# A feed-forward block's weight sums and gated differences change places between PSUM and SBUF, and their low halves change engines

## The chip, the cores and the metric

The kernel runs on one core of one Trainium2 chip. The metric is the device time of one execution in microseconds (us), given as the median of several runs. An execution covers the whole inference step, not the changed part alone.

## What is computed

One layer of a streaming encoder over 1088 frames (1024 of a prompt, 64 of a sample), all in fp32. The change lies in the two feed-forward blocks, one at the start of the layer and one at its end:

```python
def _swiglu(x, g, w_in, w_out):
    a, b = jnp.split(_rms(x, g) @ w_in, 2, axis=-1)
    return (jax.nn.silu(a) * b) @ w_out

h = x + 0.5 * _swiglu(x, ffn1_norm, ffn1_w_in, ffn1_w_out)
...   # attention with top-k keys, a convolution branch, gates, an output projection
h = h + 0.5 * _swiglu(h, ffn2_norm, ffn2_w_in, ffn2_w_out)
```

The model width is 1024 and the inner width of the feed-forward blocks is 2816, which is 22 tiles of 128.

## The kernel before, in words

**Products.** Each fp32 operand is kept as two fp32r tiles, a rounded high half and a low half that holds the remainder. `split` (lines 151 to 156) makes them: ScalarE (ACT) copies the high half (L155), and VectorE (DVE) or GpSimd (POOL) subtracts it from the operand (L156). [...] A product of two such operands is three matmuls (`mm3`): high weight by high data (L139), high weight by low data (L140), low weight by high data (L141). So the matmul of L141 is the first that needs a weight's low half.

**Seven products for eight.** Both phases of a feed-forward block use a Strassen-Winograd scheme: of a 2x2 block product, seven block products are formed instead of eight, from sums and differences of the blocks. Operands 0 and 1 are plain weight blocks, 2 to 6 are made of sums. The data operands are made once per half of the frames by `prep`; the weight operands are made for every use by `wops`.

**Weights, `wops`.** Two blocks of 128x1024 (`ra`, `rb`; 512 KB each) are loaded by SyncE's DMA queue into a ring of three buffers (`wraw`, `NRAW = 3`). With `a11` set, `halves` splits `ra` as a whole (L374 on ACT, L375 on POOL), which gives operands 0 and 1. Then four sums of 128x512 follow: `s[0]` is copied by ACT (L358) and completed by DVE (L360), `s[2]` is L359, `s[1]` is L362, `s[3]` is L365. Operand 4 is made of `s[0]`, 2 of `s[1]`, 3 of `s[2]`, 6 of `s[3]`, 5 of the raw block `b1`. L365 is DVE's last reading of `ra`, and POOL's low half of operand 5 the last reading of `rb`. The second buffer of the next pair is the one that held `ra`, so its load waits for L365, and for L375 where there is one. The operands' buffers (`wp`) are a ring of six; the sums that lie in SBUF (`s`) have a ring of four; all PSUM tiles (`ps`) share eight banks of 128x512.

**Phase 1, `up`.** A unit is one tile of the inner width for half of the frames: products 0, 4, 2, 1, 3, 6, 5 in the program's order, 84 matmuls, and the additions that combine them. There are 22 units per half and block, 88 in all. The first six units of the first block have the products 0 and 1 done early (`lead`), so that 60 matmuls are left, in the order 4, 2, 6, 3, 5. At the end of a unit the two gated results, `c` and `d`, stand in two banks. Where the inner tiles come in groups of four (all but the last two groups) phase 2 uses seven products too, and the odd unit of a pair forms the sums that these need: `t2`, `t3` and `t4`, three tiles of 128x272, each split into halves (`gh`, `gl`).

**Phase 2, `down`.** It calls `wops` with `sb=True` (32 times in all), which places all sums but the first in SBUF, and adds its products to `h` on DVE (L489). Its products run in the order 0, 4, 2, 1, 3, 6, 5, and in the second feed-forward block (`late`) 0, 4, 2, 6, 3, 1, 5.

**What sets the order.** The program gives priorities (`high_priority`), and a scheduler that plays the program through a model of the engines sets one fixed order per engine. On the chip each engine works its own list strictly in that order and waits for semaphores. So an edit in one line can move instructions everywhere in the feed-forward blocks; between the two blocks the lists are the same before and after the change.

Of the kernel before, what the change touches and what calls it, by code (L numbers as in the profile page):

```python
# [9 lines left out]
F32 = mybir.dt.float32  # L10
# [6 lines left out]
ALU = mybir.AluOpType  # L17
AX = mybir.AxisListType

P = 128  # L20
# [9 lines left out]
HW = 272  # L30
# [64 lines left out]
class Kern:  # L95
# [242 lines left out]
    def wops(self, offs, a11=True, sb=False):  # L338

        nc = self.nc  # L340
        res = [None] * 7
        v = nc.vector.tensor_tensor
        with self.tc.high_priority(WAHEAD):
            ra, rb = (self.wraw.tile([P, 1024], F32, name="raw", tag="raw") for _ in range(2))
            for t, o in ((ra, offs[0]), (rb, offs[1])):
                nc.sync.dma_start(t, self.a["wf"][o:o + P * 1024].rearrange("(p n) -> p n", p=P))
            if a11:
                res[0], res[1] = self.halves(ra)
            a0, a1, b0, b1 = ra[:, 0:512], ra[:, 512:1024], rb[:, 0:512], rb[:, 512:1024]
            s = [self.wsum.tile([P, 512], F32, name="s", tag="s") if i % 2 or (sb and i) else self.psum()  # L350
                 for i in range(4)]

            def put(o, x, eng=None):
                t = self.wpart.tile([P, 1024], F32R, name="wp", tag="wp")
                res[o] = t[:, 0:512], t[:, 512:1024]
                self.split(*res[o], x, eng or self.weng)

            nc.scalar.activation(s[0], b0, AF.Copy)  # L358
            v(s[2], a0, s[0], op=ALU.subtract)  # L359
            v(s[0], s[0], b1, op=ALU.add)  # L360
            put(4, s[0], nc.vector)
            v(s[1], s[0], a0, op=ALU.subtract)  # L362
            put(2, s[1])
            put(3, s[2], None if sb else nc.vector)
            v(s[3], a1, s[1], op=ALU.subtract)  # L365
            put(6, s[3])
            put(5, b1)
        return res
# [30 lines left out]
    def up(self, w, tp, g, odd, seven, lead=None):  # L399
        nc = self.nc  # L400
        v = nc.vector.tensor_tensor
        act = nc.scalar.activation
        self.turn ^= 4
        p1, sa, u2, p5 = (self.spare[:, self.turn + i, :] for i in range(4))
        t1, g12 = sa, u2
        c22 = tp.tile([P, HW], F32, name="u3", tag="u3", bufs=2)
        if lead:
            p1, sa = lead
            d = self.product(w[4], 4)
            self.keep(p5, d)  # L410
            v(u2, p1, self.product(w[2], 2), op=ALU.add)
            self.product(w[6], 6, d)
            c = self.product(w[3], 3)
            v(c, u2, c, op=ALU.add)
            v(c22, c, p5, op=ALU.add)
            b = self.product(w[5], 5)
            self.keep(p5, c)
            v(c, p5, b, op=ALU.add)
        else:
            c = self.product(w[0], 0)  # L420
            self.keep(p1, c)
            d = self.product(w[4], 4)
            self.keep(p5, d)
            self.product(w[2], 2, c)
            self.keep(u2, c)
            v(sa, p1, self.product(w[1], 1), op=ALU.add)
            act(sa, sa, AF.Silu)
            self.product(w[3], 3, c)
            v(c22, c, p5, op=ALU.add)
            self.product(w[6], 6, d)  # L430
            self.product(w[5], 5, c)
        v(d, u2, d, op=ALU.add)
        act(d, d, AF.Silu)
        put = lambda o, x, eng=None: self.split(g[0][:, o, :], g[1][:, o, :], x, eng)
        if not seven:
            v(d, c22, d, op=ALU.mult)
            v(c, sa, c, op=ALU.mult)
            put(2 * odd + 1, d)
            put(2 * odd, c)
        elif not odd:  # L440
            v(g12, c22, d, op=ALU.mult)
            v(c, sa, c, op=ALU.mult)
            put(0, c)
            v(t1, g12, c, op=ALU.subtract)
            put(4, t1, nc.gpsimd)
            self.held = t1, g12
        else:
            t1, g12 = self.held
            t2, t3, t4 = (tp.tile([P, HW], F32, name="t", tag="t") for _ in range(3))
            v(d, c22, d, op=ALU.mult)  # L450
            v(t2, d, t1, op=ALU.subtract)
            put(2, t2)
            v(c, sa, c, op=ALU.mult)
            put(1, c)
            put(6, d)
            v(t3, d, g12, op=ALU.subtract)
            put(3, t3, nc.gpsimd)
            v(t4, c, t2, op=ALU.subtract)
            put(5, t4, nc.gpsimd)

# [1333 lines left out]
```

## Time and profile before

| | |
|---|---|
| median of 3 runs | 2284.51 us (2284.19 to 2287.46) |
| the profiled execution's own time | 2283.71 us |
| its span, first to last instruction | 2282.0 us |
| mean granted TensorE clock | 0.996 |
| weight operands' low halves: on DVE, on POOL | 208, 392 of 128x512 |
| low halves of `t2`, `t3` and `t4` and of the even unit's `t1`: on DVE, on POOL | 32, 96 of 128x272 |

TensorE (PE) is the busiest engine by far. Its matmuls overlap in the pipeline, so "busy" alone doesn't tell whether it runs at its full rate; the number of matmuls that start in a stretch does. The first feed-forward block takes up about 20 to 740 us of the span, the second about 1540 to 2280 us. In the timeline a row has its start in us, its length in us, engine, line, operation and tiles, and in brackets the idle time of the engine before it with what ended it. In the groups a row ends with the total busy time, the mean length of one in ns, and the idle time before.

### The profile page before, as it was taken

How to read it: one execution, taken by the hardware profiler on the slowest of the kernel's cores; microseconds unless marked ns; L12 is line 12 of the kernel's file. 1: busy time of each engine (PE TensorE's matmuls, PEld its weight loads, DVE VectorE, ACT ScalarE, POOL GpSimd, SP SyncE). 2: the span in 40 equal slices, each digit the busy share in tenths (PEclk: the TensorE clock that was granted, in tenths of full speed). 3: DMA queues.
4: the chain of work that ended last, by engine and by line, in shares of the span. 5: the costliest groups of instructions: out<-in, count | busy, mean ns of one | idle time of the engine just before them, and what ended most of it. 6: DMA issues, size and time to landing. Idle time of an engine off the chain costs nothing.

```text
span 2282.0 us, 44290 instructions
## 1 busy us (share of the span) xinstructions
PE 2238.1 (98%) x16300; PEld 2208.2 (97%) x16300; DVE 1683.1 (74%) x3809; ACT 1415.9 (62%) x2965; POOL 1447.1 (63%) x1014
## 2 busy tenths in 40 slices
PE   8999999999999999999999999999999999999998
PEld 8999999999999999999999999999999999999998
DVE  7887756777766468689965877677777667887765
ACT  7665555666546454788548888656656556555554
POOL 5677755677766595598922333477677666667766
PEclk9999999999999999999999999999999999999999
DMA  5332332333223534224322556742323232323233
GB/s 199 106 109 96 103 102 92 107 111 103 94 96 124 164 117 142 90 78 152 119 96 82 177 174 212 259 172 93 103 93 111 93 111 75 113 99 107 102 103 114
DMA packets 131643, 273.40 MB, mean 120 GB/s; under 512 B 17888, under 2 KB 81248, under 8 KB 131424
## 3 DMA queue, kind: packets, MB, share of 16 engines
q1 hardware_dynamic: 130848, 270.00, 35.8%
q8 instruction: 128, 2.10, 0.4%
q14 instruction: 91, 0.75, 0.1%
q10 hardware_dynamic: 576, 0.56, 0.1%
HBM read 231.82 MB, written 38.75 MB: 119 GB/s over the span
## 4 chain that ended last, share of the span: by engine, by line
PE 80%; DVE 4%; DMA 3%; ACT 3%; issue 2%; POOL 2%; SPq 0%; DVEq 0%; POOLq 0%; ACTq 0%
PE ps L139 25%; PE ps L141 25%; PE ps L140 25%; DMA raw<-wf 2%; POOL wp L156 1%; PE pt L1293 1%; PE lgi L1003 1%; PE lgi L1004 1%; PE ps L174 1%; PE lg L1269 1%; PE lg L1270 1%; PE pv L1314 1%; PE pv L1315 1%; ACT wp L155 0%; ACT whi L121 0%
## 5 line engine op out<-in xcount | busy, mean ns | idle before, releaser
L139 PE MATMUL ps<-x,wp 128*128 128x272 f32 x1760 | 507.3, 290 | 4.2 <-ACT wp L155 2.9
L141 PE MATMUL ps<-x,wp 128*128 128x272 f32 x1760 | 504.2, 291 | 4.1 <-POOL wp L156 2.2
L140 PE MATMUL ps<-x,wp 128*128 128x272 f32 x1760 | 506.3, 288 | 0.0
L139 PE MATMUL ps<-x,whi 128*128 128x272 f32 (+2 forms) x1544 | 480.4, 311 | 4.4 <-ACT x L155 2.4
L156 POOL TENSOR_TENSOR wp<-s,wp 128x512 fp32r<-128x512 f32 x272 | 365.2, 1355 | 183.1 <-ACT wp L155 182.0
L141 PE MATMUL ps<-x,wlo 128*128 128x272 f32 (+2 forms) x1544 | 480.1, 311 | 0.0
L122 POOL TENSOR_TENSOR wlo<-raw,whi 128x1024 fp32r<-128x1024 f32 (+1 forms) x123 | 278.5, 2267 | 291.2 <-ACT whi L121 278.6
L140 PE MATMUL ps<-x,whi 128*128 128x272 f32 (+2 forms) x1334 | 410.8, 308 | 0.0
L375 POOL TENSOR_TENSOR wlo<-raw,whi 128x1024 fp32r<-128x1024 f32 x120 | 289.6, 2414 | 180.3 <-ACT whi L374 158.5
L139 PEld LDWEIGHTS ps<-x,wp 128*128 128x128 f32 x1760 | 331.2, 188 | 7.5 <-ACT wp L155 4.7
L141 PEld LDWEIGHTS ps<-x,wp 128*128 128x128 f32 x1760 | 328.6, 188 | 7.9 <-DVE wp L156 3.8
L140 PEld LDWEIGHTS ps<-x,wp 128*128 128x128 f32 x1760 | 331.9, 189 | 0.0
L139 PEld LDWEIGHTS ps<-x,whi 128*128 128x128 f32 x1544 | 291.5, 189 | 6.5 <-ACT x L155 2.7
L141 PEld LDWEIGHTS ps<-x,wlo 128*128 128x128 f32 x1544 | 291.7, 189 | 0.9
L140 PEld LDWEIGHTS ps<-x,whi 128*128 128x128 f32 x1334 | 252.5, 189 | 1.1
L155 ACT ACTIVATE wp<-s 128x512 fp32r<-128x512 f32 x272 | 168.1, 626 | 134.2 <-DVE s L362 76.4
L844 POOL TENSOR_TENSOR ac<-ac,pd 128x559 f32<-128x559 f32 (+1 forms) x132 | 193.1, 1464 | 25.1 <-ACT pd L843 18.2
L155 ACT ACTIVATE wp<-ps 128x512 fp32r<-128x512 f32 x208 | 123.1, 592 | 113.3 <-DVE ps L360 102.6
L489 DVE SCALAR_TENSOR_TENSOR h<-ps,h 128x272 f32<-128x272 f32 x448 | 174.9, 430 | 14.8 <-PE ps L141 13.6
L140 PE MATMUL ps<-gl,whi 128*128 128x272 f32 x640 | 183.5, 291 | 0.4 <-DVE gl L156 0.4
L140 PE MATMUL ps<-gl,wp 128*128 128x272 f32 x640 | 180.7, 288 | 0.4 <-POOL gl L156 0.4
L139 PE MATMUL ps<-gh,whi 128*128 128x272 f32 x640 | 176.5, 292 | 4.6 <-DVE spare L332 2.2
(314 smaller groups left out, 5807.9 us busy)
## 6 DMA issues: line engine op xcount, KB each, us to landing
raw<-wf SPq DMA_DIRECT2D x353, 512.0 KB, 3.3
d_g<-sg SPq DMA_DIRECT2D x32, 181.0 KB, 1.9
gc<-d_g SPq DMA_DIRECT2D x32, 181.0 KB, 3.4
raw<-wf SPq DMA_DIRECT2D x16, 256.0 KB, 2.7
raw<-d_q SPq DMA_DIRECT2D x32, 128.0 KB, 3.7
y<-t SPq DMA_DIRECT2D x24, 136.0 KB, 1.9
raw<-d_qi SPq DMA_DIRECT2D x24, 128.0 KB, 3.0
d_g<-sg SPq DMA_DIRECT2D x16, 182.0 KB, 3.4
```

The costliest lines, as they stand in the source:

```text
L122: self.weng.tensor_tensor(lo[:, :n], raw[:, :n], hi[:, :n], op=ALU.subtract)
L139: t.matmul(out, wh, xh, start=first, stop=False, skip_group_check=onto)
L140: t.matmul(out, wh, xl, start=False, stop=False, skip_group_check=onto)
L141: self.mm = t.matmul(out, wl, xh, start=False, stop=last, skip_group_check=onto).ins
L155: nc.scalar.activation(hi, x, AF.Copy)
L156: (eng or nc.vector).tensor_tensor(lo, x, hi, op=ALU.subtract)
L174: self.nc.tensor.matmul(ps[:, b * P:(b + 1) * P], x[:, t0:t0 + P], self.ones, start=i == 0, stop=i == len(tiles) - 1)
L375: self.weng.tensor_tensor(lo, raw, hi, op=ALU.subtract)
L489: nc.vector.scalar_tensor_tensor(x, p, 0.5, x, op0=ALU.mult, op1=ALU.add)
L844: nc.gpsimd.tensor_tensor(ac, ac, pd, op=ALU.add)
L1003: nc.tensor.matmul(o, qt[:, hd, :], kih[:, ks:ks + pw], start=True, stop=False)
L1004: nc.tensor.matmul(o, qt[:, hd, :], kil[:, ks:ks + pw], start=False, stop=True)
```

## The change

The change has two parts, and both leave the number of operations on each engine as it was.

In `wops` of phase 1 (`sb` false, 88 calls) `s[1]` goes from SBUF to a PSUM bank and `s[2]` from a bank to SBUF. The low half of operand 2, which is made of `s[1]`, goes from POOL to DVE, and the low half of operand 3 from DVE to POOL. With `sb` true the four sums and their engines stay as they were.

In `up`, in the odd unit of a pair (32 of them), `t3` is no longer a tile of its own: the difference is written over `d` in its bank, after `d` itself has been split (operand 6). The low half of `t3` goes from POOL to DVE, and the low half of `t2`, which stays in SBUF, from DVE to POOL.

```diff
-            s = [self.wsum.tile([P, 512], F32, name="s", tag="s") if i % 2 or (sb and i) else self.psum()
+            s = [self.wsum.tile([P, 512], F32, name="s", tag="s") if i > 1 or (sb and i) else self.psum()
                  for i in range(4)]
...
             v(s[1], s[0], a0, op=ALU.subtract)
-            put(2, s[1])
-            put(3, s[2], None if sb else nc.vector)
+            put(2, s[1], None if sb else nc.vector)
+            put(3, s[2])
             v(s[3], a1, s[1], op=ALU.subtract)
...
-            t2, t3, t4 = (tp.tile([P, HW], F32, name="t", tag="t") for _ in range(3))
+            t2, t4 = (tp.tile([P, HW], F32, name="t", tag="t") for _ in range(2))
             v(d, c22, d, op=ALU.mult)
             v(t2, d, t1, op=ALU.subtract)
-            put(2, t2)
+            put(2, t2, nc.gpsimd)
             v(c, sa, c, op=ALU.mult)
             put(1, c)
             put(6, d)
-            v(t3, d, g12, op=ALU.subtract)
-            put(3, t3, nc.gpsimd)
+            v(d, d, g12, op=ALU.subtract)
+            put(3, d)
             v(t4, c, t2, op=ALU.subtract)
             put(5, t4, nc.gpsimd)
```

**DVE, second lead unit of the first block.** These are DVE's rows from the unit's L359 to its second low half (L156) in the kernel before. `raw_723` is `ra`, `ps_727` is `s[0]`, `s_728` is `s[1]`, `ps_729` is `s[2]`; the rows with `spare` or `u3` belong to the unit ahead of it.

```order
L359 TENSOR_TENSOR ps_729<-raw_723,ps_727 128x512
L360 TENSOR_TENSOR ps_727<-ps_727,raw_724 128x512
L411 TENSOR_TENSOR spare_87<-gf_301,ps_655 128x272
L414 TENSOR_TENSOR ps_681<-spare_87,ps_681 128x272
L432 TENSOR_TENSOR ps_641<-spare_87,ps_641 128x272
L156 TENSOR_TENSOR wp_734<-ps_727,wp_734 128x512
L362 TENSOR_TENSOR s_728<-ps_727,raw_723 128x512
L415 TENSOR_TENSOR u3_640<-ps_681,spare_87 128x272
L365 TENSOR_TENSOR s_730<-raw_723,s_728 128x512
L441 TENSOR_TENSOR spare_87<-u3_640,ps_641 128x272
L156 TENSOR_TENSOR wp_741<-ps_729,wp_741 128x512
```

And these are the same unit's rows now, with `s_729` for `s[2]` and `ps_728` for `s[1]`.

```order
L359 TENSOR_TENSOR s_729<-raw_723,ps_727 128x512
L360 TENSOR_TENSOR ps_727<-ps_727,raw_724 128x512
L432 TENSOR_TENSOR ps_641<-spare_87,ps_641 128x272
L418 TENSOR_TENSOR ps_681<-spare_87,ps_696 128x272
L156 TENSOR_TENSOR wp_734<-ps_727,wp_734 128x512
L362 TENSOR_TENSOR ps_728<-ps_727,raw_723 128x512
L442 TENSOR_TENSOR ps_681<-gf_301,ps_681 128x272
L441 TENSOR_TENSOR spare_87<-u3_640,ps_641 128x272
L156 TENSOR_TENSOR wp_738<-ps_728,wp_738 128x512
L365 TENSOR_TENSOR s_730<-raw_723,ps_728 128x512
```

L365 stood ahead of the second low half, with one row between it and L362; it now stands behind it, with three rows between. L411, L414 and L415 have moved ahead of L359. Over all 88 phase-1 units the mean distance from L359 to L365 in DVE's list goes from 7.7 to 9.5 rows.

**POOL, the first odd unit.** POOL's rows before, from the low half of a whole raw block (`wlo`) to the two low halves of gated differences (`t_825` is `t3`, `t_826` is `t4`):

```order
L375 TENSOR_TENSOR wlo_963<-raw_958,whi_962 128x1024
L156 TENSOR_TENSOR wp_862<-s_852,wp_862 128x512
L156 TENSOR_TENSOR wp_869<-s_854,wp_869 128x512
L156 TENSOR_TENSOR wp_872<-raw_848,wp_872 128x512
L156 TENSOR_TENSOR gl_611<-t_825,gh_610 128x272
L156 TENSOR_TENSOR gl_611<-t_826,gh_610 128x272
```

The same place now (`wp_864` is operand 3 of the weights, `t_824` is `t2`, `t_825` is `t4`):

```order
L375 TENSOR_TENSOR wlo_962<-raw_957,whi_961 128x1024
L156 TENSOR_TENSOR wp_864<-s_852,wp_864 128x512
L156 TENSOR_TENSOR gl_611<-t_824,gh_610 128x272
L156 TENSOR_TENSOR wp_868<-s_853,wp_868 128x512
L156 TENSOR_TENSOR wp_871<-raw_847,wp_871 128x512
L156 TENSOR_TENSOR gl_611<-t_825,gh_610 128x272
```

Behind the low half of the whole block stands operand 3 where operand 2 stood, and the low half of `t2` is now ahead of the low halves of the operands 6 and 5.

**DVE, a phase-1 unit of the last block near 2040 us of the span.** Before, from the first low half to the second:

```order
L156 TENSOR_TENSOR wp_26499<-ps_26492,wp_26499 128x512
L362 TENSOR_TENSOR s_26493<-ps_26492,raw_26483 128x512
L489 SCALAR_TENSOR_TENSOR h_18892<-ps_26348,h_18892 128x272
L426 TENSOR_TENSOR spare_19436<-spare_19436,ps_26558 128x272
L365 TENSOR_TENSOR s_26495<-raw_26483,s_26493 128x512
L156 TENSOR_TENSOR wp_26506<-ps_26494,wp_26506 128x512
```

Now, the same unit:

```order
L489 SCALAR_TENSOR_TENSOR h_18876<-ps_26320,h_18876 128x272
L156 TENSOR_TENSOR wp_26471<-ps_26464,wp_26471 128x512
L362 TENSOR_TENSOR ps_26465<-ps_26464,raw_26455 128x512
L156 TENSOR_TENSOR wp_26475<-ps_26465,wp_26475 128x512
L365 TENSOR_TENSOR s_26467<-raw_26455,ps_26465 128x512
L359 TENSOR_TENSOR s_26608<-raw_26597,ps_26606 128x512
```

The low half of operand 2 (`wp_26475`) has come to DVE and stands right behind L362, ahead of L365.

## The prediction

> **What bounds the kernel now.** I read the page's first part, then the busy times by stretch of 57 us, then TensorE's waits, and last the timeline where it waits.
>
> ```profile
> span 2282.0 us, 44290 instructions
> PE 2238.1 (98%) x16300; PEld 2208.2 (97%) x16300; DVE 1683.1 (74%) x3809; ACT 1415.9 (62%) x2965; POOL 1447.1 (63%) x1014
> ```
> ```profile
> 57.00:114.00 57.00, 55.58 (x420) 53.22 (x419) 50.13 (x123) 34.97 (x79) 37.10 (x28) 1.00 0.31 106
> ...
> 171.00:228.00 57.00, 57.00 (x456) 57.00 (x455) 43.86 (x89) 33.72 (x74) 42.04 (x30) 1.00 0.28 97
> ...
> 1995.00:2052.00 57.00, 54.90 (x429) 53.74 (x428) 47.56 (x106) 31.25 (x70) 36.15 (x26) 1.00 0.28 99
> 2052.00:2109.00 57.00, 55.98 (x438) 54.89 (x437) 45.79 (x90) 33.05 (x74) 41.50 (x30) 1.00 0.31 107
> ```
> Columns two and three are TensorE's busy time with the matmuls started and that of its weight loads; DVE, ACT and POOL follow. At 171 us 456 matmuls start in 57 us, one each 0.125 us, and TensorE never idles: that is its full rate, and no edit to another engine makes such a stretch shorter. What the change can move is the rest: 36 starts are missing at 57 us, 27 and 18 in the last two rows (a few per cent of them may be records that were lost), 4.5, 3.4 and 2.3 us.
>
> ```profile
> PE ps L139 <- ACT wp L155: 3.5, 4, 2.0
> PE ps L141 <- POOL wp L156: 2.2, 5, 1.2
> PE ps L141 <- DVE wp L156: 1.8, 8, 0.3
> ```
> The columns are us in total, times, and the longest. TensorE's waits for phase-1 weights come to 7.5 us, 0.3% of the time. The longest one for POOL:
>
> ```profile
> 2042.42 0.29 PE L140 MATMUL ps<-x,wp 128*128 128x272 f32 x1
> 2043.88 0.40 PE L141 MATMUL ps<-x,wp 128*128 128x272 f32 x1 [1.18 <-POOL wp L156]
> 2044.12 0.29 PE L139 MATMUL ps<-x,wp 128*128 128x272 f32 x1
> ```
> ```profile
> 2038.40 2.41 POOL L375 TENSOR_TENSOR wlo<-raw,whi 128x1024 fp32r<-128x1024 f32 x1 [4.61 <-ACT whi L374]
> 2042.21 2.89 POOL L156 TENSOR_TENSOR wp<-s,wp 128x512 fp32r<-128x512 f32 x2 [1.40 <-ACT wp L155]
> ```
> A product began with its high half, and its third matmul waited for the low half that POOL was making. By the order of POOL's list this is operand 2, the one that the change gives to DVE.
>
> **Where the weights are late: the ring of raw buffers.** The other waits lie mostly in the six lead units.
>
> ```profile
> 45.90 0.60 ACT L358 ACTIVATE ps<-raw 128x512 f32<-128x512 f32 x1 [1.23 <-DMA raw<-wf]
> ...
> 50.27 0.63 ACT L155 ACTIVATE wp<-s 128x512 fp32r<-128x512 f32 x1 [0.86 <-DVE s L362]
> ...
> 54.35 0.60 ACT L358 ACTIVATE ps<-raw 128x512 f32<-128x512 f32 x1 [0.74 <-DMA raw<-wf]
> ```
> ```profile
> 47.14 0.69 DVE L360 TENSOR_TENSOR ps<-ps,raw 128x512 f32<-128x512 f32 x1
> ...
> 48.90 0.68 DVE L156 TENSOR_TENSOR wp<-ps,wp 128x512 fp32r<-128x512 f32 x1
> 49.50 0.68 DVE L362 TENSOR_TENSOR s<-ps,raw 128x512 f32<-128x512 f32 x1
> ...
> 50.45 0.68 DVE L365 TENSOR_TENSOR s<-raw,s 128x512 f32<-128x512 f32 x1
> ...
> 51.42 0.69 DVE L156 TENSOR_TENSOR wp<-ps,wp 128x512 fp32r<-128x512 f32 x1
> ```
> ```profile
> SPq L346 <- DVE s L365: 21.1, 4, 8.4
> ```
> ```profile
> raw<-wf SPq DMA_DIRECT2D x353, 512.0 KB, 3.3
> ```
> L365 ends at 51.13, the load that waited for it takes the 3.3 us of the DMA row, and the next unit starts at 54.35: a cycle of 8.45 us, against 60 matmuls of 0.125 us, 7.5 us. Here TensorE loses about 0.95 us a unit, and what ends last is the cycle load, L358, DVE's sums, L365.
>
> **The change part by part.** The counts stay, so I cost kinds of operations first.
>
> ```profile
> L365 DVE TENSOR_TENSOR s<-raw,s 128x512 f32<-128x512 f32 x120 | 113.7, 948 | 1.9
> L360 DVE TENSOR_TENSOR ps<-ps,raw 128x512 f32<-128x512 f32 x120 | 83.0, 692 | 0.0
> L362 DVE TENSOR_TENSOR s<-ps,raw 128x512 f32<-128x512 f32 x120 | 81.5, 679 | 0.0
> L156 DVE TENSOR_TENSOR wp<-ps,wp 128x512 fp32r<-128x512 f32 x208 | 142.7, 686 | 45.7 <-ACT wp L155 43.7 <-PE ps L141 0.8
> L156 POOL TENSOR_TENSOR wp<-s,wp 128x512 fp32r<-128x512 f32 x272 | 365.2, 1355 | 183.1 <-ACT wp L155 182.0 <-PE ps L141 0.6
> L156 DVE TENSOR_TENSOR gl<-ps,gh 128x272 fp32r<-128x272 f32 x144 | 62.3, 433 | 25.3 <-ACT gh L155 24.6
> L156 DVE TENSOR_TENSOR gl<-t,gh 128x272 fp32r<-128x272 f32 x32 | 30.7, 961 | 6.0 <-ACT gh L155 6.0
> L156 POOL TENSOR_TENSOR gl<-t,gh 128x272 fp32r<-128x272 f32 x64 | 52.7, 829 | 26.3 <-ACT gh L155 18.4 <-DVE h L489 5.8 <-DVE t L458 1.3
> ```
> DVE is slow in just the two forms with both inputs in SBUF: 948 ns against 679 to 692 for the same size with one in a bank, 961 against 433 in the halves. Both go from phase 1: L365 gets a bank for one input (88 times 0.26 us, 23 us), and the low half on DVE is that of a bank (32 times 0.53 us, 17 us). DVE's 1683 us fall by 40 us, to some 1643. POOL and ACT do as many operations as before at the same prices. For ACT's high halves of swapped places I take nothing, since each kind is as frequent after as before.
>
> [...] In the rows, L362 with an input in a bank takes 679 ns and the longest of the bank forms 692. [...]
>
> Of DVE's 40 us nearly all is hidden, because in the full stretches TensorE covers it. The terms that reach the end:
>
> (a) Operand 2's low half on DVE. It costs 0.69 us there instead of 1.36 and no longer queues behind the 2.41 us of the whole block on POOL; operand 3 takes that place, one or two products later (1.5 us each, 12 matmuls), which is its cover. I take all five POOL waits, 2.2 us, and for each the slower step behind it (0.24 us from 2043.88 to 2044.12 where 0.125 is usual), 0.1: 2.7 us less. Ends: 0, if operand 2's high half turns out last, and 3.3, were the step twice as dear.
>
> (b) L365 behind operand 2's low half. That low half needs ACT's high half after L362: 0.68 + 0.63 = 1.31 us after L362 starts, then 0.69, so L365 starts 2.0 us after L362 instead of 0.95, 1.05 later. Queued behind the waiting low half on DVE are L365 and the sums of the unit ahead; who waits for L365 is the next load. One small row less stands between L360 and the first low half (at most 0.40 us back, its high half being done at about 48.5). So the cycle grows by 0.65 to 1.05 us, over three lead units 2.0 to 3.2. Against that, the second operand that TensorE takes up is complete 2.0 us after L362's start, where operand 3 was complete at 51.42 + 0.69 - 49.50 = 2.6; and the fourth unit's products 0 and 1, 24 matmuls or 3.0 us, need no sum. I take 1.0 us per group of three lead units, 2.0 us more for both; ends 0 and 6.4.
>
> (c) Outside the lead units the same delay meets slack: a unit of 84 matmuls takes 10.5 us, the cycle about 9.5 with the delay. Two of the four waits for ACT's high half lie where a half of the frames has just begun, and the slack is gone:
>
> ```profile
> 408.07 0.39 PE L139 MATMUL ps<-x,wp 128*128 128x272 f32 x1 [1.95 <-ACT wp L155]
> ```
> ```profile
> 2025.82 0.40 PE L139 MATMUL ps<-gh,wp 128*128 128x272 f32 x1 [0.54 <-ACT wp L155]
> ```
> At the first I take 0.5 us more, ends 0 and 2 for both.
>
> (d) Blocked subtractions on the cycle.
>
> ```profile
> 2051.01 2.79 DVE L365 TENSOR_TENSOR s<-raw,s 128x512 f32<-128x512 f32 x1
> ```
> This one took 2.79 us instead of 0.68, in one of the two late stretches of the table above. It gives back 2.1 us, less the 1.05 of (b) and, by guess, half of the rest for what TensorE has in store: 0.5 us less, ends 0 and 2.1.
>
> (e) `d` stays in its bank until its second pair of halves is done.
>
> ```profile
> L358 ACT ACTIVATE ps<-raw 128x512 f32<-128x512 f32 x120 | 72.1, 601 | 93.2 <-DMA raw<-wf 69.8 <-DVE t L456 15.6 <-DVE ry L202 2.7
> L155 ACT ACTIVATE gh<-ps 128x272 fp32r<-128x272 f32 x144 | 55.8, 389 | 33.4 <-DVE ps L437 16.5 <-DVE ps L436 11.9 <-DVE ps L453 4.1
> ```
> ACT's L358 already waits 15.6 us in all for L456, which reads `d` last; now 0.39 and 0.43 us come behind it, 0.8 to 1.7 us with rows between. ACT's high halves queue behind L358. The full stretches hide it; I take 0, ends 0 and 2 (two such waits uncovered). The low half of `t2` moves ahead of operands 6 and 5 on POOL, 0.8 us of that engine, with the same cover: 0, ends -0.5 and 1.
>
> Sum: -2.7 + 2.0 + 0.5 - 0.5 = -0.7 us on the profiled execution's 2283.7 (span 2282.0 and 1.7 around it), 2283.0. The median of the runs is 0.8 above that execution, so I forecast **2283.8 us**.
>
> **The rivals.**
>
> *Faster: the blocked DVE was what held the weights back.* For it: L365's mean is 0.27 us above its free length, and it is on the cycle. The stretches where TensorE falls short, 57 to 171 and 1995 to 2109, hold 228 of some 1460 us of feed-forward, 16%: of DVE's 40 us 6.4 fall there. If they all shorten the cycle, with (a), 9.1 us go: 2275.4. Against it: at 45 to 55 us L365 took its free 0.68, so the lead units have nothing to win. What makes it likely at all is that two-input forms alone are slow. [...] Chance 0.24.
>
> *Slower: the ring.* If TensorE finds no cover in the lead units, (b) costs its 6.4 us, and with 0.5 of (c), 2 of (e) and (a) used up by operand 3 arriving late on POOL, the time is 2284.5 + 8.9 = 2293.4; with (a) kept, 2290.7. It decides once the cycle's delay over three units passes the 3.0 us of products 0 and 1. For it: DVE's list has L365 1.8 rows later on average over all units. Against it: the second operand's 0.6 us. Chance 0.26.
>
> *The change doesn't do what it says:* operand 2's low half is held by ACT's high half, ready at 2042.2 where POOL had waited for it too, and the waits change their name alone. Then (a) is 0.5 at most and the time 2284 to 2286. Chance 0.10.
>
> **How the numbers follow.** A measurement of this kernel tells about 0.2% (4.6 us) from no change. My own case, within it, has 0.40. Same: 0.40 + 0.10 = 0.50; faster 0.24; slower 0.26. The bounds of the terms alone give about -7 to +9; the range 2277.0 to 2291.0 takes in most of both rivals and leaves out 2275.4 and 2293.4, some 2 in 10.
>
> **What would show it.** In the profile after: TensorE's row for POOL's weight halves at L141 gone or under 0.5 us; DVE near 1643 us, L365 at about 0.69 us in phase 1, no DVE row of `gl` from `t`; the distance of two L358 in the lead units 9.1 to 9.5 us instead of 8.45, and the starts at 57 to 114 us some 8 fewer. I'd be wrong if that distance stayed at 8.45, if the full stretches lost starts, or if the time left 2279.9 to 2289.1.

## The result, and the profile after

| | median, us | runs | lowest to highest | ratio, 95% interval |
|---|---|---|---|---|
| before | 2284.35 | 6 | 2282.85 to 2287.46 | |
| after | 2303.81 | 6 | 2302.52 to 2307.43 | 1.0086, 1.0075 to 1.0097 |

The change makes the kernel 19.5 us slower. The forecast was 2283.8, a little faster, with a range of 2277.0 to 2291.0, so it was wrong in sign and the range didn't hold the time.

The first lines of the page after, which answer to the two shown of before:

```profile
span 2302.2 us, 44286 instructions
PE 2243.2 (97%) x16300; PEld 2207.0 (96%) x16300; DVE 1650.4 (72%) x3809; ACT 1422.2 (62%) x2965; POOL 1429.9 (62%) x1014
```

DVE's busy time did fall, by 32.7 us, and the time rose all the same. The groups of DVE show that the prices of the single operations were right:

```profile
L362 DVE TENSOR_TENSOR ps<-ps,raw 128x512 f32<-128x512 f32 x88 | 60.7, 690 | 0.0
L365 DVE TENSOR_TENSOR s<-raw,ps 128x512 f32<-128x512 f32 x88 | 59.6, 677 | 0.0
L365 DVE TENSOR_TENSOR s<-raw,s 128x512 f32<-128x512 f32 x32 | 31.3, 978 | 0.4
...
L156 DVE TENSOR_TENSOR gl<-ps,gh 128x272 fp32r<-128x272 f32 x176 | 76.4, 436 | 43.3 <-ACT gh L155 41.1
```

L365 takes 677 ns with one input in a bank and 978 where both are still in SBUF; its 113.7 us became 59.6 + 31.3 = 90.9. The low halves of the gated differences took 62.3 + 30.7 = 93.0 and take 76.4. Together 39.4 us less, as reckoned. (The page's busy time fell by less, to 1650.4 us and not to 1643, since DVE's other lines became longer by 5.6 us in all, none of them by more than 1.2.)

TensorE's waits for phase 1's weights, of after, in us in total, times and longest:

```profile
PE ps L139 <- ACT wp L155: 7.4, 9, 2.3
PE ps L139 <- ACT gh L155: 4.3, 5, 1.1
PE ps L139 <- ACT spare L390: 4.3, 6, 1.0
...
PE ps L141 <- POOL wp L156: 1.8, 5, 0.5
PE ps L141 <- DVE wp L156: 1.1, 5, 0.2
```

And two of the same rows before:

```profile
PE ps L139 <- ACT gh L155: 2.0, 3, 0.8
PE ps L139 <- ACT spare L390: 0.6, 3, 0.2
```

The waits for POOL's low halves, 2.2 us, were to go; 1.8 are there. The waits for ACT's high halves of the weights, 3.5 us, became 7.4, and those for ACT's high halves of the data and its copies rose from 2.6 to 8.6 together.

The stretches of 57 us show starts that are gone, in the first block's lead units and outside them. After, in three stretches, then the last of them before (the other two of before are in the prediction):

```profile
57.00:114.00 57.00, 52.98 (x395) 50.12 (x393) 47.65 (x116) 32.59 (x73) 33.61 (x26) 1.00 0.30 102
171.00:228.00 57.00, 57.00 (x455) 57.00 (x454) 41.85 (x90) 34.60 (x74) 39.66 (x29) 1.00 0.29 97
228.00:285.00 57.00, 55.91 (x442) 55.46 (x442) 39.00 (x83) 35.41 (x77) 37.57 (x28) 1.00 0.29 99
```
```profile
228.00:285.00 57.00, 57.00 (x456) 57.00 (x456) 43.64 (x94) 33.37 (x73) 40.27 (x30) 1.00 0.30 103
```

At 57 us 25 starts are gone where the prediction had 8. The stretch at 228 us was full before, with 456 starts, and has 442 after: a full stretch lost starts, which the prediction had named as a sign that it is wrong. (After is 7 to 9 us behind at that place; what stands there was in full stretches before all the same.)

Where the time went is seen best by taking the n-th matmul of one trace and the n-th of the other (both have 16300; the order differs in places, so this compares progress by count). This table is worked out so from the starts of TensorE's matmuls:

| the matmul that started before at | 40.32 | 68.67 | 85.01 | 97.05 | 128.75 | 171.01 | 300.09 | 410.03 | 734.48 | 1474 | 2275 |
|---|---|---|---|---|---|---|---|---|---|---|---|
| starts after later by, us | 0.8 | 2.3 | 3.8 | 4.6 | 5.5 | 7.0 | 9.3 | 10.4 | 10.7 | 12.0 | 20.4 |

The first block loses 10.7 us, the stretch between the blocks about 1, the second block about 8. At 40.32 us stands the first matmul with a weight made of sums, so the 0.8 us there arose ahead of all that was edited. The matmuls of the lead units run from 40 to 69 us and from 97 to 129: they lose some 1.5 and 0.9 us. The rest of the first block's loss, some 7.5 us, arises in units outside the lead.

The second lead unit after, from ACT's list and from DVE's, against the rows of before in the prediction:

```profile
47.61 0.60 ACT L358 ACTIVATE ps<-raw 128x512 f32<-128x512 f32 x1 [1.84 <-DMA raw<-wf]
...
51.53 0.60 ACT L155 ACTIVATE wp<-ps 128x512 fp32r<-128x512 f32 x1 [1.07 <-DVE ps L362]
...
56.82 0.60 ACT L358 ACTIVATE ps<-raw 128x512 f32<-128x512 f32 x1 [1.52 <-DMA raw<-wf]
```
```profile
50.81 0.69 DVE L362 TENSOR_TENSOR ps<-ps,raw 128x512 f32<-128x512 f32 x1
...
52.17 0.69 DVE L156 TENSOR_TENSOR wp<-ps,wp 128x512 fp32r<-128x512 f32 x1
52.77 0.68 DVE L365 TENSOR_TENSOR s<-raw,ps 128x512 f32<-128x512 f32 x1
```

L365 starts 1.96 us after L362 (0.95 before), ends at 53.45, and the next unit starts 3.37 us later, at 56.82. The distance of two L358 is 9.2 us where it was 8.45. In the six lead units the distances are 9.2 to 10.1 us, where they were 8.4 to 9.9. So far this is the prediction's step (b), in its size too.

Outside the lead, this is a place near 248 us, in ACT's list, DVE's and TensorE's:

```profile
244.74 0.40 ACT L155 ACTIVATE gh<-ps 128x272 fp32r<-128x272 f32 x1
248.05 0.60 ACT L358 ACTIVATE ps<-raw 128x512 f32<-128x512 f32 x1 [2.91 <-DMA raw<-wf]
248.59 0.41 ACT L155 ACTIVATE gh<-spare 128x272 fp32r<-128x272 f32 x1
248.90 0.38 ACT L390 ACTIVATE spare<-ps 128x272 f32<-128x272 f32 x1
```
```profile
241.59 0.69 DVE L156 TENSOR_TENSOR wp<-ps,wp 128x512 fp32r<-128x512 f32 x1 [1.04 <-ACT wp L155]
242.20 0.68 DVE L365 TENSOR_TENSOR s<-raw,ps 128x512 f32<-128x512 f32 x1
```
```profile
249.33 0.39 PE L139 MATMUL ps<-x,wp 128*128 128x272 f32 x1 [0.84 <-ACT spare L390]
```

DVE stands at operand 2's low half for 1.04 us, L365 comes behind it and ends at 242.88, and the load that it releases is there for L358 at 248.05. ACT stands at L358 for 2.91 us. L390, a copy that empties one of TensorE's banks, is queued behind it, and TensorE waits 0.84 us for that. (A load that takes 5.1 us is an exception here; in the median L358 starts 3.3 us after L365 ends where it waits for the load.) All over the trace ACT's L358 waits more for its load. The loads don't wait for L365 more often, but longer in total. These are the two rows of after, then the second one of before (the first is in the prediction, 69.8 us for the load):

```profile
L358 ACT ACTIVATE ps<-raw 128x512 f32<-128x512 f32 x120 | 72.2, 601 | 113.3 <-DMA raw<-wf 99.3 <-DVE h L489 7.9 <-PE ps L141 3.2
```
```profile
SPq L346 <- DVE s L365: 249.2, 43, 16.4
```
```profile
SPq L346 <- DVE s L365: 172.5, 46, 15.3
```

### The profile page after: what moved, and what is told of

Its sections match the earlier page's. It is cut to its first block, busy times and chain, and to the rows that moved or that the text cites. A ratio compares the mean times of both kernels' runs of the same rounds, so it can differ in the third digit from the quotient of the medians.

```text
span 2302.2 us, 44286 instructions
## 1 busy us (share of the span) xinstructions
PE 2243.2 (97%) x16300; PEld 2207.0 (96%) x16300; DVE 1650.4 (72%) x3809; ACT 1422.2 (62%) x2965; POOL 1429.9 (62%) x1014
## 4 chain that ended last, share of the span: by engine, by line
PE 72%; DVE 9%; DMA 6%; POOL 5%; issue 4%; ACT 3%; SPq 0%; POOLq 0%; DVEq 0%; ACTq 0%
PE ps L139 22%; PE ps L141 22%; PE ps L140 22%; DMA raw<-wf 4%; POOL wp L156 3%; POOL wlo L375 1%; DVE h L489 1%; PE pt L1293 1%; ACT wp L155 1%; DVE wp L156 1%; PE lgi L1003 1%; PE lgi L1004 1%; PE ps L174 1%; DMA d_mp<-gc 1%; DVE ps L360 1%
## 5 line engine op out<-in xcount | busy, mean ns | idle before, releaser
L141 PE MATMUL ps<-x,wp 128*128 128x272 f32 x1760 | 506.0, 291 | 3.0 <-POOL wp L156 1.8
L156 POOL TENSOR_TENSOR wp<-s,wp 128x512 fp32r<-128x512 f32 x272 | 358.5, 1330 | 222.9 <-ACT wp L155 208.8
L141 PE MATMUL ps<-x,wlo 128*128 128x272 f32 (+2 forms) x1544 | 479.9, 311 | 0.0
L141 PEld LDWEIGHTS ps<-x,wp 128*128 128x128 f32 x1760 | 329.4, 188 | 6.4 <-POOL wp L156 3.7
L141 PEld LDWEIGHTS ps<-x,wlo 128*128 128x128 f32 x1544 | 291.4, 189 | 0.9
```

Source lines behind the costliest of these rows:

```text
L141: self.mm = t.matmul(out, wl, xh, start=False, stop=last, skip_group_check=onto).ins
L156: (eng or nc.vector).tensor_tensor(lo, x, hi, op=ALU.subtract)
```

## The experiments

The theories. **R**, the raw ring: L365 comes later, it frees the raw buffer, and L358 of the next unit, with all that stands behind it on ACT, comes later with it. **G**: the gated part holds the bank of `d` longer. **S**: the sums' part costs something beside L365's place (in the last three runs: the ring is covered, and the halves and their order set the time). **N**: the lists that the scheduler made for before are good ones, and nearly any other order costs several us. Eleven kernels were run. "Cycle" is the mean over the 120 units from the start of L358 to the end of L365 (the k-th L358 of the trace with the k-th L365); "idle" is ACT's idle time at L358 that ended with the raw load. The ratio is to the kernel before as measured beside each on its chip (medians 2284.05, 2284.17 and 2285.67).

| kernel | cycle, us | idle, us | median, us | ratio to before, 95% interval |
|---|---|---|---|---|
| before | 5.95 | 69.8 | 2284.35 | |
| after | 6.61 | 99.3 | 2303.81 | 1.0075 to 1.0097 |
| sums' part alone | 6.79 | 99.3 | 2310.62 | 1.0098 to 1.0129 |
| gated part alone | 6.01 | 66.0 | 2290.56 | 1.0015 to 1.0041 |
| after, L365 ahead of both halves | 5.99 | 50.9 | 2300.31 | 1.0056 to 1.0084 |
| before, L365 late | 7.46 | 108.0 | 2339.28 | 1.0229 to 1.0260 |
| after, L365 between the halves | 6.27 | 71.2 | 2292.73 | 1.0024 to 1.0049 |
| sums' part, L365 between | 6.21 | 76.7 | 2297.01 | 1.0038 to 1.0064 |
| gated part, engines only | 6.05 | 55.2 | 2291.95 | 1.0022 to 1.0049 |
| before, operands 6 and 5 exchanged | 6.44 | 117.3 | 2326.43 | 1.0169 to 1.0197 |
| before, 5 temporaries | 5.96 | 69.2 | 2289.77 | 1.0007 to 1.0026 |
| before, 4 raw buffers | 6.26 | 36.7 | 2280.12 | 0.9971 to 0.9988 |
| after, 4 raw buffers | 6.91 | 40.3 | 2284.85 | 0.9991 to 1.0009 |

**The two parts alone.** The first is the change's edits to `wops` on the kernel before, the second its edits to `up`.

> Only the part in the weight sums is done (second sum in a bank, third in SBUF, low halves swapped); the gated differences are as before. Theory R (raw ring: the low half of operand 2 now stands ahead of L365 on DVE, so ra is freed and the next pair loaded later): nearly the whole loss is here, 2299 to 2306 us, the lead units' distance of two L358 about 9.2 to 9.7 us. Theory G (the gated difference keeps its bank longer and t2's low half queues on POOL): as before, 2282 to 2287. Theory N (any new order of the lists costs, wherever L365 stands): 2292 to 2306, without a longer L358 distance.

> Only the part in the gated differences is done (third difference over its bank, low halves swapped); the weight sums are as before. Theory R: 2282 to 2288 us, since L365 stands where it stood (2.5 rows behind L362 on average). Theory G: 2298 to 2306, nearly the whole loss. Theory N: 2292 to 2306.

The sums alone cost 26.6 us (2310.62), more than the whole change, and the gated part alone 6.5 (2290.56). Most of the loss comes with the sums. Both times lie outside all the ranges of R, G and N. The whole change costs less than its first part alone, so the parts are not terms that add up.

**L365 late in the kernel before.** Nothing of the change is in it; only L365 of phase 1 is put behind the low half of operand 3 in DVE's list:

```diff
-            v(s[3], a1, s[1], op=ALU.subtract)
+            if sb:
+                v(s[3], a1, s[1], op=ALU.subtract)
+            else:
+                with self.tc.issue_after(self.lo):
+                    v(s[3], a1, s[1], op=ALU.subtract)
```

(`self.lo` is the last low half that `split` wrote.)

> The kernel before, with one edit of the order: in phase 1 L365 is queued behind the low half of operand 3 on DVE (4.6 rows behind L362 instead of 2.5); banks and engines as before. Theory R: the loss comes without any change of bank or engine, 2298 to 2312 us, lead distance 9.3 to 10 us. Theory G: 2282 to 2287. Theory N: 2292 to 2306 without a longer distance.

```profile
L358 ACT ACTIVATE ps<-raw 128x512 f32<-128x512 f32 x120 | 72.2, 602 | 133.6 <-DMA raw<-wf 108.0 <-DVE t L460 9.4 <-DVE h L493 6.3
```

2339.28, 55 us more, with the cycle 1.5 us longer. A late L365, with the lists that the scheduler makes around it, is enough for a loss larger than that of the change. But 55 us is far above R's 2298 to 2312, and L365 became longer too (1108 and 1377 ns on average in its two forms, 948 before), so the size isn't the place's alone.

**L365 early in the changed kernel.** In `wops` the line of L365 goes ahead of the halves of operand 2:

```diff
             v(s[1], s[0], a0, op=ALU.subtract)
+            v(s[3], a1, s[1], op=ALU.subtract)
             put(2, s[1], None if sb else nc.vector)
             put(3, s[2])
-            v(s[3], a1, s[1], op=ALU.subtract)
```

> The changed kernel with the fourth sum (L365's subtraction) written ahead of the second operand's halves: banks and engines as in the changed kernel, the subtraction 2.9 rows behind L362 instead of 4.4 (before: 2.5). Theory R: the loss goes, 2279 to 2288 us, lead distance back to 8.4 to 8.8 us. Theory G: stays at 2300 to 2306. Theory N: stays at 2292 to 2306.

The cycle is back at 5.99 us and ACT's idle below that of before, yet only 3.5 us came back. As a test of R this kernel has a fault of its own, which its row on ACT shows:

```profile
52.00 0.60 ACT L155 ACTIVATE wp<-ps 128x512 fp32r<-128x512 f32 x1 [0.76 <-DVE s L363]
```

This is the high half of operand 2. It needs L362 alone, but here it starts when L363 (the L365 of this kernel) has ended. On average over the 120 units it ends 6.55 us after L358 starts, where it was 5.30 in the changed kernel. So one lateness was exchanged for another, now on the second operand that TensorE takes up, and TensorE waits more for ACT's high halves than in the changed kernel (7.4 us):

```profile
PE ps L139 <- ACT wp L155: 10.6, 11, 2.9
```

R's time, 2279 to 2288, was missed all the same, and since the edit did two things at once, the run decides neither for R nor against it.

**L365 between the two halves of operand 2.** ACT's high half is written first, then L365, then DVE's low half; the rest is the changed kernel, and in a second run the sums' part alone.

```diff
+                nc.scalar.activation(res[2][0], s[1], AF.Copy)
+                v(s[3], a1, s[1], op=ALU.subtract)
+                v(res[2][1], s[1], res[2][0], op=ALU.subtract)
                 put(3, s[2])
```

> The changed kernel, in phase 1 with ACT's high half of operand 2 first, then L365, then operand 2's low half on DVE: L365 no longer queues behind the low half, and, unlike the run with L365 written ahead of both halves (2300.3), no high half has to wait for L365. Theory R, the ring of raw buffers (a late L365 is the loss): start of L358 to end of L365 back to about 6.0 us, ACT's idle at L358 for the raw load back to some 65 to 75 us, operand 2's high half at about 5.3 us after L358 as now; the sums' part of the loss (13 of 19.5 us) goes and only the gated difference's 6.5 stays: 2290, 2286 to 2294. Theory S, the sums' swap itself (operand 3 later on POOL, the bank): L358 to L365 as for R, but the time stays at 2298 to 2304. Theory N, any new order costs some: in between, without relation to the distance.

> The kernel before with the sums' part of the change alone (2310.6 when L365 queued behind operand 2's low half), now with L365 between ACT's high half and DVE's low half of operand 2. Theory R: all of the 26.6 us was L365's place: 2284, 2280 to 2288, with L358 to L365's end at about 6.0 us. Theory S: 2296 or more. Theory N: between, 2287 to 2296.

The changed kernel comes down by 11 us to 2292.73, as R had it. The sums' part alone comes down by 13.6 to 2297.01, half of what R wanted; that time is one that S had named, 2296 or more. The cycle went only part of the way back, half in the first run (6.27 us) and some two thirds in the second (6.21), so L365's lateness was not fully undone; whether the rest of the second run is R or S, these two don't decide.

**The gated part, engines only.** Operand 2's low half goes to POOL and operand 3's to DVE, with `t3` still a tile in SBUF:

```diff
-            put(2, t2)
+            put(2, t2, nc.gpsimd)
...
-            put(3, t3, nc.gpsimd)
+            put(3, t3)
```

> The kernel before with only the engines of two low halves swapped in the gated product (operand 2's on POOL, operand 3's on DVE); the second difference stays in a tile in SBUF, so its bank is free as early as before. Theory G, the bank held longer is what the gated part costs (6.5 us): 2284, 2281 to 2287. If the swap of the engines costs it (the low halves' new places in the two lists): 2290, 2287 to 2293.

2291.95: the cost of the gated part is there without the bank, so G falls. What the two runs share is the exchange of the engines, with the new places of the low halves in the lists.

**A new order and nothing else.** In the kernel before, the lines of operands 6 and 5 change places:

```diff
-            put(6, s[3])
             put(5, b1)
+            put(6, s[3])
```

> The kernel before, with operands 6 and 5 of phase 1's weights written in the other order and nothing else: a new order of DVE's, ACT's and POOL's lists without any change of an operation, a bank or an engine. Theory N (any other order than the one the kernel has costs several us): 2288 to 2300. Theories R and G (only the places that they name cost): rb is freed one half earlier and L365 is as before, 2284, 2281 to 2288.

2326.43, 42 us more, far beyond what any theory gave. N is true at least in this: an order that looks harmless can cost more than the change. But it isn't without relation to the ring, since the idle at the load rose to 117.3 us (it doesn't give the size of a loss, though: 99.3 us stand beside losses of 19.5 and 26.6). And one row shows an operation that grew though nothing of it was edited:

```profile
L365 DVE TENSOR_TENSOR s<-raw,s 128x512 f32<-128x512 f32 x120 | 152.6, 1272 | 1.7
```

L365 takes 1272 ns on average, 948 before.

**A fourth raw buffer.** These runs leave L365 where it is and take away what makes it matter. In the first block every fourth raw tile comes from a pool of its own, so that a load waits for the L365 of the unit before the last. The room for it comes from one of six temporaries, and the first run is the control for that. (The new helper moves all line numbers by 6 in the last two kernels; their L364 is L358.)

```diff
+    def rawt(self):
+        self.nr += 1
+        p = self.xraw if self.xraw is not None and self.nr % 4 == 0 else self.wraw
+        return p.tile([P, 1024], F32, name="raw", tag="raw")
...
-            tp = self.pool(ff, "tp1", 6)
+            tp = self.pool(ff, "tp1", 5)
...
+            self.xraw = self.pool(ffw, "wrawx", 1)
```

> The kernel before with 5 instead of 6 buffers in the pool of temporaries of both feed-forward blocks, and nothing else: the control for the next two, which need the room. 2284 to 2292 on any theory; what it costs is to be taken off the next two.

> The kernel before with 5 temporaries and, in the first feed-forward block alone, a fourth raw buffer, so that a load waits for the L365 of the unit before the last and no longer for the last one. Theory R (ring): ACT's idle at L358 for the raw load falls from 70 to 40 us or less (the second block's share stays), and the time falls against the control by 2 to 8 us. Theory S (the ring is hidden, the high and low halves and their order set the time): same as the control within 2 us.

> The changed kernel with 5 temporaries and the fourth raw buffer in the first block alone. The change cost 10.7 us in the first block and some 8 in the second. Theory R: the first block's part is gone but for the gated half (0 to 4 us against the kernel before with four raw buffers at the same matmul), the whole difference to that kernel is 8 to 12 us. Theory S: the first block still costs 8 to 12 us against that kernel, the whole 16 to 22. If the times of these two lie apart by an amount that the first block doesn't show, it is the second block's.

The control lies in its range. The kernel before gains 9.7 us on it with the fourth buffer, where R had 2 to 8 and S nothing. The changed kernel lies 4.7 us above that one, where R had 8 to 12 and S 16 to 22. So both are nearer to R, and both gained more than R had.

The groups of the last two, the kernel before and the changed one, each with four raw buffers:

```profile
L364 ACT ACTIVATE ps<-raw 128x512 f32<-128x512 f32 x120 | 71.5, 596 | 65.7 <-DMA raw<-wf 36.7 <-DVE t L462 16.4 <-DVE h L495 4.1
```
```profile
L364 ACT ACTIVATE ps<-raw 128x512 f32<-128x512 f32 x120 | 71.6, 596 | 50.7 <-DMA raw<-wf 40.3 <-PE ps L147 3.1 <-DVE h L495 3.0
```

These are of the whole trace. The same groups in the first 760 us alone, which is the first block, in four kernels: before, after, before with four buffers, after with four buffers.

```profile
L358 ACT ACTIVATE ps<-raw 128x512 f32<-128x512 f32 x60 | 36.1, 602 | 46.6 <-DMA raw<-wf 33.9 <-DVE t L456 8.8 <-DVE h L489 2.3
```
```profile
L358 ACT ACTIVATE ps<-raw 128x512 f32<-128x512 f32 x60 | 36.1, 602 | 64.3 <-DMA raw<-wf 59.9 <-DVE h L489 2.9 <-DVE t L458 1.3
```
```profile
L364 ACT ACTIVATE ps<-raw 128x512 f32<-128x512 f32 x60 | 35.6, 593 | 14.4 <-DVE t L462 8.9 <-DVE h L495 4.1 <-DVE t L464 0.9
```
```profile
L364 ACT ACTIVATE ps<-raw 128x512 f32<-128x512 f32 x60 | 35.5, 592 | 5.4 <-DVE h L495 2.4 <-DVE t L464 1.2 <-DVE gl L162 1.0
```

In the first block ACT's idle for the load rose from 33.9 to 59.9 us with the change. With the fourth buffer it is gone in both kernels (0.0 and 0.3 us); all that the rows of the whole trace still show is the second block's. TensorE's waits for ACT's high halves of the weights, 7.4 us in the changed kernel, are down too:

```profile
PE ps L145 <- ACT wp L161: 1.7, 2, 1.4
```

And one matmul near the end of the first block, at the same place of TensorE's list in four kernels: before, after, before with four buffers, after with four buffers.

```profile
734.25 0.39 PE L139 MATMUL ps<-gh,whi 128*128 128x272 f32 x1 [0.73 <-ACT gh L155]
```
```profile
744.97 0.39 PE L139 MATMUL ps<-gh,whi 128*128 128x272 f32 x1 [1.09 <-ACT gh L155]
```
```profile
729.51 0.40 PE L145 MATMUL ps<-gh,whi 128*128 128x272 f32 x1 [0.73 <-ACT gh L161]
```
```profile
726.41 0.39 PE L145 MATMUL ps<-gh,whi 128*128 128x272 f32 x1 [0.74 <-ACT gh L161]
```

With three buffers the change costs 10.7 us up to this matmul, with four it gains 3.1. The 3.1 is not to be taken as a gain: each trace is one execution, these two lie 2.3 us above and 1.9 below their kernels' medians, and between the blocks, where TensorE's list is the same in all, two traces drift apart by up to 5.6 us. That the 10.7 us are gone is clear of this, and the medians agree: the change costs 19.5 us with three buffers in both blocks and 4.7 with four in the first (2284.85 less 2280.12). In that last kernel the cycle from L358 to L365 is the longest of the four, 6.91 us on average; it is late and no longer matters. So the first block's loss comes through the raw ring, and S, which had 8 to 12 us left there, falls for it. The lists of the two kernels with four buffers are new ones as well, and how much of their times is N isn't separated. For the gated part by itself it isn't shown either: it was not run with four buffers, and with three ACT's idle for the load was below that of before (66.0 and 55.2 us against 69.8). Of the second block, which kept three buffers, the comparison says that its loss stays: some 6 us between the same two traces from 1474 us on.

The kernel before with the fourth buffer, 2280.12, is faster than both kernels: 5.5 us below the 2285.67 that before gave beside it on that chip, and 9.7 below its own control. So the ring held the kernel before back as well.

## Why the prediction was wrong

**What bounds the kernel** was read rightly, the ring of raw buffers and the cycle load, L358, DVE's sums, L365. But it was read as a matter of the six lead units. Its own row had ACT idle at L358 for the raw load for 69.8 us in the whole trace, of which only 4.7 lie at the six lead units (6.4 of 99.3 after). The same wait stood at half of the 120 units, and after at two thirds, as the waits of before and of after show (us in total, times, longest):

```profile
ACT ps L358 <- DMA raw<-wf: 69.8, 61, 3.3
```
```profile
ACT ps L358 <- DMA raw<-wf: 99.3, 79, 3.7
```

**(a) Operand 2's low half on DVE, -2.7 us.** Nearly none of it came. The waits for POOL at L141 went from 2.2 us to 1.8: five before, all in operand 2's product, and five after, all in operand 3's. The cover of "one or two products" was not there; that it was lost because all of a unit's weights came later is likely, not shown.

**(b) L365 behind operand 2's low half, lead units, +2.0 us.** Right: L365 1.96 us after L362 (2.0 reckoned), a distance of 9.2 to 9.6 us in the first group and 9.2 to 10.1 in the second (9.1 to 9.5), and some 2.4 us lost in the two groups by the table of matmuls. In the lead units rows of the unit ahead fill DVE's wait for the high half; outside them it can stand bare, as the 1.04 us of the row at 241.59.

**(c) "Outside the lead units the same delay meets slack", +0.5 us. This is the step that failed.** It set a mean unit of 10.5 us against a cycle of 9.5 with the delay and called the difference slack. The 9.5 was the lead units' own cycle; outside them L358's start to L365's end takes 5.98 us on average before and 6.63 after, with the load's 3.3 a cycle of 9.9. That is still under 10.5, and the loss came all the same: about 7.5 us in the first block outside the lead units and some 8 more in the second, where the step had 0.5. The place at 248 us shows why: from the start of the unit's L358 at 235.57 it took 12.48 us to the next, since L365 ended 7.31 us after that start and the load wasn't there for another 5.17, not the usual 3.3.

```profile
235.57 0.60 ACT L358 ACTIVATE ps<-raw 128x512 f32<-128x512 f32 x1 [1.84 <-DMA raw<-wf]
```

A ring of three buffers holds a unit and a half, so as I read it a unit that runs long can't be made up by one that runs short: little can be loaded ahead. With a fourth buffer ACT's idle for the load went from 59.9 us to 0.3 in the first block, and the loss of that block with it. So the slack of the mean isn't there unit by unit; the wait at L358 was already common, and such a unit passes the delay on. Then ACT, standing at L358, held back the copies and high halves behind it, which is how the delay reached TensorE at 249 us; TensorE's longer waits for ACT, above, fit it.

**(d) Blocked subtractions freed, -0.5 us.** The operations are free, 677 ns on average for L365 with a bank. It was of no use, because L365 had to wait before it could start: its start moved from 1.24 to 2.16 us after L362 on average, more than the 0.27 us that its length lost.

POOL's low halves of the gated differences, of after, became shorter too (829 ns before):

```profile
L156 POOL TENSOR_TENSOR gl<-t,gh 128x272 fp32r<-128x272 f32 x64 | 49.2, 778 | 4.8 <-ACT gh L155 4.6
```

Counted from the starts and ends in the two traces, 10 of these 64 overlap an L365 before, and take 1108 ns on average; the other 54 take 777. After, none of the 64 overlaps an L365 with two SBUF inputs. L365 itself takes 943 to 1377 ns on average with two SBUF inputs, in the kernel before, the changed one and nine of the eleven runs, and 677 to 686 with one in a bank.

**(e) The gated part, 0.** Alone it costs 6.5 us, but not by the mechanism of this step: it costs as much with the bank freed early. With four raw buffers the changed kernel, this part in it, has no loss in the first block.

**The bounds.** The ends of the terms add up to -5.9 and +11.4 us, not to "about -7 to +9". Even the upper one gives no more than 2295.9.

**The rivals.** "The ring" had the sign and the mechanism, at 2293.4, and a lower chance than the forecast; it too put the loss into the lead units and stayed 10 us short. The point that it gave, when the delay over three units passes 3.0 us, is not the one that decided. "The blocked DVE" had the operations right and their effect on the time wrong. "The change doesn't do what it says" was right that waits for ACT's high halves would take the place of those for POOL's low halves, but its time, 2284 to 2286, had no loss in it.

**What stays open.** Why the order 5, 6 makes L365 so much longer where it meets POOL, and how much of its 42 us is that. Which wait in the gated part's new lists makes its 6.5 us, and whether that is the ring. How much of each run's time is the new order of its lists alone. Whether the second block would be cured by a fourth buffer too: it wasn't tried.

## What to carry to other kernels

Before costing a delay on an operation that frees a buffer, look at how often the load behind it is what ends a wait, over the whole trace. Here it was so in half of the units (61 of 120); the slack that the means promised was not there, and the in-order engine that waited for the load passed the delay on to what stood behind it (ACT's 2.91 us at L358 near 248 us, then 0.84 us of TensorE). Shorter operations on an engine that is 74% busy brought nothing here (DVE's busy time fell by 32.7 us, and the kernel became 19.5 us slower), since the change put the one that frees a buffer behind a waiting one; a further buffer in the ring was worth more than the edit (9.7 us less than its control), and it took away the edit's loss in its block.

## What was not expected of the hardware

A change of order alone, with the same operations in the same places, made one of them a third longer (L365, 948 to 1272 ns): in these traces the length of L365 with its two SBUF inputs goes with whether POOL is busy at that time. Before, 27 of the 120 L365 have no POOL instruction beside them in the trace, and the longest of these takes 694 ns; the other 93 take 1023 on average, the longest 2924. With operands 6 and 5 exchanged it is 20 with at most 693 ns, and 100 with 1389 on average. After, all 88 L365 with one input in a bank have POOL beside them, and the longest takes 680; their mean stayed within 677 to 686 ns in all the runs that have them.
